# Expert weights stored by partition and column half, gathers that pass over empty places, and a landing allowance for the first expert

## The chip, the cores and the metric

One core of a Trainium2 chip runs the whole program in a single launch. The metric is the device time of that launch in microseconds, taken as the median of several executions; lower is better. One further execution was recorded by the hardware profiler, and the rows below come from that one. The engines are called as the profile calls them: PE (matrix), PEld (its weight load), DVE (vector), ACT (scalar), POOL (GpSimd) and SP (sync, which issues most DMAs).

## What is computed

A decoder layer over 2048 tokens of width 1024: an input projection, three parallel mixers (stick-breaking attention with 8 heads, a gated recurrence, a convolution module), an output projection, and then a mixture of experts. Only the last part matters here:

```python
logits_c = h @ w_coarse                      # 4 groups, take the best
logits_f = h @ w_fine                        # 8 experts a group, take the best two of the group
gate = softmax(top_val) * w_grp
# every token goes to 2 of 32 experts:
y[tok] += gate * ((silu(x[tok] @ w_gate[e]) * (x[tok] @ w_up[e])) @ w_down[e])
```

`w_gate` and `w_up` are 1024 x 512 for each expert, `w_down` is 512 x 1024, all float32: 2 MB each, 6 MB an expert, some 201 MB for 32 experts.

## The kernel before

**One plan for the whole program.** `Plan` collects every step as an `Op` with an engine, a cost, its reads and writes and a wished time, and then writes out a fixed order for every engine. `schedule` does it `ROUNDS` = 4 times: `forward` is a list scheduler that fills the engines by priority, `backward` runs the same from the end and gives every op a new priority (the latest end that it may have), so that the next `forward` follows other priorities everywhere; the best of the four orders is issued. On the chip each engine works through its own list in that order: an instruction whose input is late holds up whatever stands behind it on the same engine. A step that starts a DMA (`nb` bytes) is taken to land at `DMA0 + nb / DMAR + DMA1` after its issue, in ns; for one 512 KB piece of weights these constants come to 3.2 us.

**The order of the work.** The projection comes first, then attention. From attention's last steps on, the 16 token tiles of 128 tokens pass through `tok_tile` (norms, output projection L1286 to L1288, residual L1295, the second norm: square L1308 on ACT, root L1317 and L1319 on POOL, scaling L1335 on DVE, transposes L1354 on PE, router logits) and `route` (choice of experts, and a scatter of every token's place into the table `tab`, L1576). `provisional` looks at the counts after 12 of the 16 tiles and fixes one expert as the first (r = 0), so that its weights can be loaded, and its first 128 tokens worked on, while the last four tiles are still being routed. `order` ranks the others when routing is complete.

**An expert (`moe`).** Every expert has a fixed number of places (`ROOM`: from 256 down to 96, together 4864 places for 2048 x 2 = 4096 assignments); a place without a token has index 2048 or above and gate 0. For each expert, `reg` reads its number into an SP register, and twelve pieces of 512 KB are loaded: `gu` eight of gate and up, `dn` four of down. `piece` issues the DMA into one of the raw buffers (four, F5 to F8, for the first expert; eight later) on SP (L1743), lets ACT (`hi_act`, L388) or POOL (`hi_pool`, L391) round it to a high part and DVE (`lo`, L394) take the rest as a low part. `gather` loads the expert's slice of the table (L1796) and fetches the token rows, 4 KB each, by an indirect DMA from POOL (L1799); `split` transposes them on PE (L1818) and splits them. `down` ends in an indirect DMA that adds the rows to the output (L1964).

**Two ways through gate and up.** Where an expert has 129 to 192 places (`wide`, 15 experts, 120 pieces), `gate_up_wide` keeps the weights stationary, four K blocks by 256 columns a piece; there one DMA piece is, for each partition, four runs of 256 floats (1 KB). The other 17 experts (136 pieces, 20 tiles of at most 128 tokens) go through `gate_up`: the tokens are stationary and the weights move, two K blocks by all 512 columns a piece; there a piece is two runs of 2 KB for each partition, and the 256 rows of a piece lie in a row in HBM. A piece of down is one run of 4 KB.

`wts` and the rings tie experts to each other: a high or low buffer is written again when PE has done with the piece twelve places earlier, a raw buffer when DVE has.

Of the kernel before, what the change touches and what calls it, by code (L numbers as in the profile page):

```python
# [9 lines left out]
F32 = mybir.dt.float32  # L10
F32R = mybir.dt.float32r
BF16 = mybir.dt.bfloat16
I32 = mybir.dt.int32
# [6 lines left out]
P = 128  # L20
D = 1024
S = 2048
KD = D // P
NH = 8
HD = 64
NE = 32
# [53 lines left out]
TABLE = 1283  # L80
ROUNDS, LOOK = 4, 179.658
# [50 lines left out]
class Op:  # L132
    __slots__ = ("eng", "cost", "fn", "nb", "tab", "prio", "deps", "outs", "n", "ready", "end", "idx", "label", "start", "lk", "soft")


class Plan:
# [17 lines left out]
    def op(self, eng, cost, fn, r=(), w=(), nb=0, late=0, tab=None, lk=False, after=None):  # L154
        o = Op()
        o.eng, o.cost, o.fn, o.nb, o.tab, o.lk = eng, cost, fn, nb, tab, lk
# [97 lines left out]
    def forward(self, look):  # L254
# [3 lines left out]
        for o, push in self.pick([o for o in self.ops if not o.n], look):  # L258
# [4 lines left out]
            for p in o.outs:  # L263
                p.ready = max(p.ready, o.end if p.soft == o.idx else dma + DMA1 if o.nb else o.end + LAT[o.eng][p.eng])
                p.n -= 1
                if not p.n:
                    push(p.ready, p)
# [4 lines left out]
    def backward(self):  # L272
        for o in self.ops:
            o.n, o.ready, o.prio = len(o.outs), 0, -o.end
        for o, push in self.pick([o for o in self.ops if not o.n], 0):
            for i in o.deps:
                p = self.ops[i]
                p.ready = max(p.ready, o.end + (0 if o.soft == i else DMA0 + p.nb / DMAR + DMA1 if p.nb
# [32 lines left out]
class Kern:  # L311
# [1380 lines left out]
    def moe(self, TE, TX, TW, T5):  # L1692
# [43 lines left out]
        def piece(r, src, view):  # L1736
# [7 lines left out]
                         nb=1 << 19)  # L1744
# [15 lines left out]
        N2 = lambda ap: ap.rearrange("p (k f) -> p k f", k=2)  # L1760

        def gu(r, i0, i1):
            w = wts.setdefault(r, ([], [], []))
            for q in range(i0, i1):
                if not wide(r):
# [3 lines left out]
                        bass.ds(regs[r], 1), k * 256:(k + 1) * 256, :].rearrange("o (k p) f -> p (o k) f", p=P), N2))  # L1769
# [4 lines left out]
                    bass.ds(regs[r], 1), kh * 512:(kh + 1) * 512, fp * 256:(fp + 1) * 256].rearrange(  # L1774
                        "o (k p) f -> p (o k) f", p=P), K4))
# [6 lines left out]
        def gather(g):  # L1782

            r = g["r"]
# [3 lines left out]
            for off, n, at0 in ((g["off"], g["na"], (0,)), (g["off"] + P, g["nb"], (0, HD))):  # L1788
# [6 lines left out]
                for p0 in at0:  # L1795
# [5 lines left out]
                    in_offset=bass.IndirectOffsetOnAxis(ap=sl[:n, 0:1].bitcast(I32), axis=0)), sk[:1] + hs, (x,),  # L1801
# [25 lines left out]
        def gate_up(g):  # L1827
# [6 lines left out]
            for k in range(KD):  # L1834
                ps = [w[m][k // 2] for m in range(2)]

                def f(k=k, ps=ps):
                    for ac, (hi, lo) in zip(acc, ps):
                        wh, wl = (N2(v())[:, k % 2] for v in (hi, lo))
                        xh, xl = xv(k)[:, k % 4, 0], xv(k)[:, k % 4, 1]  # L1840
                        nc.tensor.matmul(ac()[:n], xh, wh, start=(k == 0), stop=False)  # L1841
                        nc.tensor.matmul(ac()[:n], xh, wl, start=False, stop=False)  # L1842
                        nc.tensor.matmul(ac()[:n], xl, wh, start=False, stop=(k == KD - 1))  # L1843
# [192 lines left out]
    def overflow(self):  # L2036
        nc, tc, a, scr = self.nc, self.tc, self.a, self.scr
        with ExitStack() as ctx:
# [3 lines left out]
            with tc.For_i(0, n, 1) as i:  # L2042
# [17 lines left out]
                for nm in ("wg", "wu"):  # L2060
                    w = sb.tile([P, KD, 512], F32, name=nm)
                    nc.sync.dma_start(w, a[nm][bass.ds(e, 1)].rearrange("o (k p) f -> p (o k) f", p=P))
# [130 lines left out]
```

## Time and profile before

| | us |
|---|---|
| median of 3 runs | 2123.84 |
| lowest, highest | 2121.97, 2129.23 |
| the profiled execution, its own time | 2134.14 |
| its span, first to last instruction | 2132.5 |

The page gives busy time by engine, a strip of the span in 40 slices, DMA queues, the chain that ended last and the costliest groups. Matmuls are pipelined, so a busy PE need not be PE at its peak; the granted clock says at which of two levels it ran (1.00 is 2.4 GHz, 0.50 is 1.2 GHz). The mean DMA share can pass 1, since packets in flight on one engine overlap.

### The profile page before, as it was taken

What the parts mean: (1) busy time and instruction counts of PE and PEld (TensorE: products, weight loads), DVE (VectorE), ACT (ScalarE), POOL (GpSimd) and SP (SyncE); (2) the same over time, 40 slices, a digit from 0 to 9 for tenths busy, and PEclk for the clock granted to TensorE, in tenths of its full rate; (3) what the DMA queues carried; (4) which work ended last, traced back from release to release, by engine and by line L of the source; (5) the groups of instructions that cost most, each with busy time, mean ns of one, the idle gap of its engine ahead of it and who ended that gap; (6) DMA issues with size and microseconds to landing.
All of it is one profiled execution on the core that took longest, in us unless ns stands there. A gap on an engine that the chain in (4) does not pass through costs nothing. (4 is left out here: it accounts for less than half of the span.)

```text
span 2132.5 us, 34284 instructions
## 1 busy us (share of the span) xinstructions
PE 1978.0 (93%) x10871; PEld 1644.3 (77%) x10871; DVE 1729.3 (81%) x2450; ACT 1270.4 (60%) x2332; POOL 1333.6 (63%) x1299
## 2 busy tenths in 40 slices
PE   6799998999889999999999977999999999999997
PEld 4678886888667887788888756778898887988776
DVE  7985579956799999898898757668898977888785
ACT  5434554456688988688787533446555555655554
POOL 6654777558876676766676533336676765757664
PEclk9899999999999999999999988999999999999999
DMA  5431361324875554578676556898999999999995
GB/s 185 155 111 55 114 183 60 134 84 134 238 225 158 170 162 142 115 202 231 187 212 192 147 130 195 288 280 262 300 305 313 302 311 283 323 288 283 295 310 136
DMA packets 316326, 437.21 MB, mean 205 GB/s; under 512 B 29424, under 2 KB 200816, under 8 KB 316144
## 3 DMA queue, kind: packets, MB, share of 16 engines
q1 hardware_dynamic: 303792, 395.12, 59.8%
q0 software_dynamic: 12352, 39.89, 8.1%
q8 instruction: 87, 1.43, 0.3%
q14 instruction: 95, 0.78, 0.1%
HBM read 360.95 MB, written 73.96 MB: 204 GB/s over the span
## 5 line engine op out<-in xcount | busy, mean ns | idle before, releaser
L394 DVE TENSOR_TENSOR R<-F,R 128x1024 fp32r<-128x1024 f32 (+1 forms) x390 | 493.0, 1285 | 111.9 <-ACT R L388 56.5
L874 PE MATMUL B<-R,R 128*128 128x512 f32 x1920 | 471.3, 402 | 33.4 <-DVE R L498 16.6
L874 PEld LDWEIGHTS B<-R,R 128*128 128x128 f32 x1920 | 363.6, 192 | 119.0 <-DVE R L498 18.3
L1050 POOL TENSOR_TENSOR F<-F,O 128x512 f32<-128x512 f32 (+2 forms) x320 | 314.0, 991 | 155.0 <-DVE O L1042 142.2
L391 POOL TENSOR_SCALAR R<-F 128x1024 fp32r<-128x1024 f32 (+2 forms) x181 | 200.5, 1116 | 157.7 <-DMA F<-in_wu 26.3
L1888 PE MATMUL B<-R,R 128*128 128x288 f32 (+3 forms) x960 | 269.1, 355 | 7.2 <-DVE O L1906 7.2
L388 ACT ACTIVATE R<-F 128x1024 fp32r<-128x1024 f32 (+1 forms) x209 | 210.0, 1022 | 75.9 <-DMA F<-in_wg 30.9
L1042 DVE TENSOR_TENSOR_SCAN O<-O,O,B 128x513 f32<-128x513 f32 x192 | 241.1, 1270 | 14.8 <-ACT O L1027 7.1
L1890 PE MATMUL B<-R,R 128*128 128x144 f32 (+3 forms) x960 | 217.9, 247 | 0.0
L1025 ACT ACTIVATE F<-B 128x512 f32<-128x512 f32 (+2 forms) x320 | 176.4, 555 | 56.2 <-PE B L1015 30.4
L1086 DVE TENSOR_TENSOR R<-B,R 128x512 fp32r<-128x512 f32 (+1 forms) x336 | 185.8, 572 | 20.8 <-ACT R L1078 19.6
L1078 ACT ACTIVATE R<-B 128x512 fp32r<-128x512 f32 (+1 forms) x336 | 172.9, 533 | 49.4 <-PE B L1070 40.8
L1888 PEld LDWEIGHTS B<-R,R 128*128 128x128 f32 x960 | 179.7, 194 | 10.6 <-issue 8.1
L1890 PEld LDWEIGHTS B<-R,R 128*128 128x128 f32 x960 | 183.5, 196 | 0.9
L1027 ACT ACTIVATE O<-B 128x512 f32<-128x512 f32 (+2 forms) x320 | 177.8, 559 | 0.2 <-PE B L1015 0.2
L1070 PE MATMUL B<-ident,F 128*128 128x128 f32 x1088 | 171.5, 276 | 2.7 <-DVE R L1086 2.4
L1964 POOL DMA_INDIRECT out<-F,sl x50 | 98.5, 1969 | 91.4 <-DVE F L1961 32.8
L1014 PE MATMUL B<-R,R 128*128 128x512 f32 (+2 forms) x320 | 131.5, 411 | 22.5 <-DMA R<-k 7.6
L1070 PEld LDWEIGHTS B<-ident,F 128*128 128x128 f32 x1088 | 129.2, 142 | 24.3 <-DVE R L1086 7.3
L394 DVE TENSOR_TENSOR R<-O,R 128x1024 fp32r<-128x1024 f32 x94 | 123.3, 1321 | 16.5 <-POOL R L391 12.3
L1104 PE MATMUL B<-R,R 128*128 128x256 f32 (+3 forms) x388 | 130.5, 348 | 5.1 <-DVE O L1116 4.2
L1105 PE MATMUL B<-R,R 128*128 128x256 f32 (+3 forms) x424 | 130.4, 320 | 0.7 <-DVE R L1086 0.6
(355 smaller groups left out, 4778.2 us busy)
## 6 DMA issues: line engine op xcount, KB each, us to landing
F<-in_wg SPq DMA_DIRECT2D x112, 512.0 KB
F<-in_wd SPq DMA_DIRECT2D x96, 512.0 KB
R<-k SPq DMA_DIRECT2D x336, 128.0 KB
F<-in_wu SPq DMA_DIRECT2D x82, 512.0 KB
R<-v SPq DMA_DIRECT2D x112, 256.0 KB
O<-in_wu SPq DMA_DIRECT2D x46, 512.0 KB
F<-in_w_in SPq DMA_DIRECT2D x80, 256.0 KB
O<-in_wd SPq DMA_DIRECT2D x32, 512.0 KB
```

The source lines that it names most:

```text
L388: self.nc.scalar.activation(out, in_, AF.Identity if not isinstance(scale, float) else AF.Copy, scale=scale)
L391: self.nc.gpsimd.tensor_scalar(out, in_, 1.0, 1.0, op0=ALU.mult, op1=ALU.mult)
L394: self.nc.vector.tensor_tensor(out, in_, f32(hi), op=ALU.subtract)
L874: nc.tensor.matmul(acc(), l_, r_, start=(k == 0 and j == 0), stop=(k == KD - 1 and j == 2))
L1025: op("ACT", c_act(wd), lambda: nc.scalar.activation(w()[:, :wd], z()[:, :wd], AF.Sigmoid, scale=0.125), (z,), (w,), tab="sig")
L1027: op("ACT", c_act(wd), lambda: nc.scalar.activation(kp()[:, o:QT], z()[:, :wd], AF.Sigmoid, scale=-0.125), (z,), (kp,), tab="sig")
L1042: nc.vector.tensor_tensor_scan(qb()[:, o:][:, ::-1], k, z()[:, 0:1].to_broadcast([P, wd + 1]), init, op0=ALU.mult, op1=ALU.bypass)
L1050: op("POOL", 1.77 * wd + 130, lambda: nc.gpsimd.tensor_tensor(w()[:, :wd], w()[:, :wd], qb()[:, o + 1:], op=ALU.mult), (qb,), (w,), lk=True)
L1070: nc.tensor.transpose(tp()[:, col:col + P], w()[:, c * P:(c + 1) * P], self.ident)
L1086: op("DVE", c_dve(a1 - a0), lambda: nc.vector.tensor_tensor(wl()[:, a0:a1], tp()[:, a0:a1], f32(wh()[:, a0:a1]), op=ALU.subtract), (tp, wh ...
L1888: big = lambda **st: nc.tensor.matmul(o()[:, :2 * n], K4(hi())[:, k, js], x.rearrange("p a t -> p (a t)"), **st)
L1890: sml = lambda **st: nc.tensor.matmul(o()[:, :n], K4(lo())[:, k, js], x[:, 0], **st)
```

## The change

Three edits. First, the host stores gate and up weights as `(expert, partition, column half, K block, 256)`; the pieces, the moving operand of `gate_up` and its output view follow, and so does the overflow path. A wide piece is then one run of 4 KB for each partition, and a narrow one still two runs of 2 KB; the partitions of one expert lie 16 KB from each other. Second, the gather of token rows is given a bound of `S - 1` and told that an index above it is no error: such rows aren't fetched, and the buffer keeps what it held. The scatter at the end still covers all places. Third, the plan takes the first expert's weights to land `LAG` = 8000 ns later than its constants say, in `forward` and in `backward`; nothing on the chip waits for that, only the order written out can differ.

```diff
+LAG = 8000
...
-                p.ready = max(p.ready, o.end if p.soft == o.idx else dma + DMA1 if o.nb else o.end + LAT[o.eng][p.eng])
+                p.ready = max(p.ready, o.end if p.soft == o.idx else dma + DMA1 + o.lag if o.nb else o.end + LAT[o.eng][p.eng])
...
-                p.ready = max(p.ready, o.end + (0 if o.soft == i else DMA0 + p.nb / DMAR + DMA1 if p.nb
+                p.ready = max(p.ready, o.end + (0 if o.soft == i else DMA0 + p.nb / DMAR + DMA1 + p.lag if p.nb
...
             last[0] = op("SP", 580, lambda: nc.sync.dma_start(view(raw()), src()), (("reg", r),) + hold, (raw,),
-                         nb=1 << 19)
+                         nb=1 << 19, lag=0 if r else LAG)
...
-        N2 = lambda ap: ap.rearrange("p (k f) -> p k f", k=2)
+        N2 = lambda ap: ap.rearrange("p (g k f) -> p g k f", g=2, k=2)
...
-                        bass.ds(regs[r], 1), k * 256:(k + 1) * 256, :].rearrange("o (k p) f -> p (o k) f", p=P), N2))
+                        bass.ds(regs[r], 1), :, :, 2 * k:2 * k + 2].rearrange("o p g k f -> p (o g) k f"), N2))
...
-                    bass.ds(regs[r], 1), kh * 512:(kh + 1) * 512, fp * 256:(fp + 1) * 256].rearrange(
-                        "o (k p) f -> p (o k) f", p=P), K4))
+                    bass.ds(regs[r], 1), :, fp, 4 * kh:4 * kh + 4].rearrange("o p k f -> p (o k) f"), K4))
...
-                    in_offset=bass.IndirectOffsetOnAxis(ap=sl[:n, 0:1].bitcast(I32), axis=0)), sk[:1] + hs, (x,),
+                    in_offset=bass.IndirectOffsetOnAxis(ap=sl[:n, 0:1].bitcast(I32), axis=0),
+                    bounds_check=S - 1, oob_is_err=False), sk[:1] + hs, (x,),
...
-                        wh, wl = (N2(v())[:, k % 2] for v in (hi, lo))
+                        wh, wl = (N2(v())[:, :, k % 2] for v in (hi, lo))
...
-                        nc.tensor.matmul(ac()[:n], xh, wh, start=(k == 0), stop=False)
+                        o = ac()[:n].rearrange("p (g f) -> p g f", g=2)
+                        nc.tensor.matmul(o, xh, wh, start=(k == 0), stop=False)
...
+    halves = lambda w: np.ascontiguousarray(w.reshape(NE, KD, P, 2, 256).transpose(0, 2, 3, 1, 4))
...
-        "wg": g["exp_w_gate"][0], "wu": g["exp_w_up"][0], "wd": g["exp_w_down"][0],
+        "wg": halves(g["exp_w_gate"][0]), "wu": halves(g["exp_w_up"][0]), "wd": g["exp_w_down"][0],
```

## Rows read from the trace of the kernel before

**Rows 1.** The page: its first line, and busy time, share of the span and number of instructions of each engine (one line of five).

```profile
span 2132.5 us, 34284 instructions
...
PE 1978.0 (93%) x10871; PEld 1644.3 (77%) x10871; DVE 1729.3 (81%) x2450; ACT 1270.4 (60%) x2332; POOL 1333.6 (63%) x1299
```

**Rows 2.** Busy time of the engines in stretches: the stretch and its length, busy us (and instructions) of PE, PEld, DVE, ACT, POOL, then the granted clock, the DMA share and GB/s. 0 to 650 is the projection and early attention, 650 to 1100 attention with token tiles, 1200 to 1300 the last four token tiles, 1300 to 2133 the experts, 1400 to 2100 the experts without start and end.

```profile
0.00:650.00 650.00, 583.98 (x2708) 467.27 (x2708) 498.46 (x711) 346.83 (x574) 436.92 (x463) 0.97 0.47 141
650.00:1100.00 450.00, 433.20 (x2710) 363.32 (x2709) 410.21 (x606) 369.94 (x787) 309.69 (x323) 0.99 0.62 171
...
1200.00:1300.00 100.00, 77.09 (x417) 62.47 (x415) 64.17 (x188) 32.34 (x60) 37.56 (x52) 0.88 0.53 138
1300.00:2133.00 833.00, 787.08 (x4390) 668.05 (x4390) 667.14 (x808) 442.01 (x745) 490.28 (x406) 0.98 0.90 283
1400.00:2100.00 700.00, 674.45 (x3857) 577.99 (x3858) 587.93 (x679) 393.53 (x669) 439.78 (x364) 0.98 0.95 297
```

**Rows 3.** The chain that ended last, in order of time, cut to 1195 to 1320: start, length, what.

```profile
1222.85 17.55 DMA F<-in_wu
1240.48 1.05 POOL R L391
1241.60 1.28 POOL r L1317
1242.95 0.59 POOL r L1319
1243.57 1.29 DVE F L1335
1244.91 1.12 PE B L1354 x4
```

**Rows 4.** Timeline of SP: start, length and line of three issues of the first expert's weights (the last line is three issues in one).

```profile
1218.54 0.41 SPq L1743 DMA_DIRECT2D F<-in_wg  x1
...
1221.06 1.09 SPq L1743 DMA_DIRECT2D F<-in_wg  x1
...
1287.58 3.64 SPq L1743 DMA_DIRECT2D F<-in_wd  x3
```

**Rows 5.** Timelines of DVE, ACT, POOL and PE in 1205 to 1325: start, length, line, operation; in brackets the idle time of that engine just before, and what ended it.

```profile
1230.26 0.69 DVE L1295 TENSOR_TENSOR F<-B,F 128x512 f32<-128x512 f32 x1 [1.86 <-PE B L1288]
1238.46 1.23 DVE L394 TENSOR_TENSOR R<-F,R 128x1024 fp32r<-128x1024 f32 x1 [7.51 <-ACT R L388]
...
1237.37 1.06 ACT L388 ACTIVATE R<-F 128x1024 fp32r<-128x1024 f32 x1 [8.34 <-DMA F<-in_wg]
1238.34 1.04 ACT L1308 ACTIVATE F<-F 128x1024 f32<-128x1024 f32 x1
...
1240.98 1.06 ACT L1268 ACTIVATE R<-F 128x1024 fp32r<-128x1024 f32 x1 [1.51 <-DVE F L1262]
...
1295.60 1.06 ACT L388 ACTIVATE R<-F 128x1024 fp32r<-128x1024 f32 x1 [3.35 <-DMA F<-in_wd]
...
1240.48 1.05 POOL L391 TENSOR_SCALAR R<-F 128x1024 fp32r<-128x1024 f32 x1 [10.29 <-DMA F<-in_wu]
...
1244.91 1.12 PE L1354 MATMUL B<-ident,F 128*128 128x128 f32 x4 [13.02 <-DVE F L1335]
...
1312.94 1.97 PE L1818 MATMUL B<-ident,F 128*128 128x128 f32 x8 [0.70 <-DMA F<-h,sl]
```

**Rows 6.** Stretches of 10 us in the same place, columns as in rows 2.

```profile
1230.00:1240.00 10.00, 1.87 (x7) 1.35 (x6) 2.23 (x3) 2.10 (x3) 0.19 (x1) 0.50 0.91 122
1240.00:1250.00 10.00, 5.09 (x20) 4.29 (x21) 5.76 (x7) 2.25 (x3) 4.01 (x4) 0.60 0.90 304
```

**Rows 7.** Waits in 1400 to 2100: who waited for whom, us in total, times, longest. The two largest of PE, and the largest of DVE.

```profile
PE B L1818 <- DMA F<-h,sl: 10.0, 6, 3.3
PE B L1888 <- DVE O L1906: 7.2, 6, 2.7
...
DVE R L394 <- POOL R L391: 41.5, 29, 5.4
```

**Rows 8.** DMA queues in 1400 to 2100: queue and kind, packets, MB, share of 16 engines' time in that stretch. q1 holds the DMAs that SP issues, q0 the indirect ones of POOL.

```profile
q1 hardware_dynamic: 112079, 174.67, 74.1%
q0 software_dynamic: 9280, 32.51, 20.1%
```

**Rows 9.** The same for the queue of SP in five short stretches that hold almost one size of run: 1806 to 1812 (1 KB, wide gate and up), 1632 to 1638 (2 KB, narrow gate and up), 1417 to 1420 and 1917 to 1923 (4 KB, down), 2 to 12 (2 KB, input and projection weights, whose rows lie 8 and 10 KB apart).

```profile
q1 hardware_dynamic: 1750, 1.74, 89.4%
...
q1 hardware_dynamic: 941, 1.79, 85.0%
...
q1 hardware_dynamic: 347, 1.26, 102.6%
...
q1 hardware_dynamic: 338, 1.19, 63.0%
...
q1 hardware_dynamic: 1101, 1.87, 57.3%
```

**Rows 10.** Groups of instructions by line and shape: busy us in all, mean ns of one, idle time before them. The narrow gate and up matmul (the first of its three lines), a matmul of the down product with the same shape, and the gathers.

```profile
L1841 PE MATMUL B<-R,R 128*128 128x512 f32 x160 | 64.6, 404 | 0.0
...
L1947 PE MATMUL B<-R,R 128*128 128x512 f32 x200 | 78.7, 394 | 0.0
...
L1799 POOL DMA_INDIRECT F<-h,sl x50 | 76.5, 1530 | 59.1 <-DMA sl<-tab 29.2 <-PE B L1948 12.0 <-issue 7.0
```

More of the change, by code (lines that the diff above doesn't have):

```diff
@@ L132 @@
 class Op:
-    __slots__ = ("eng", "cost", "fn", "nb", "tab", "prio", "deps", "outs", "n", "ready", "end", "idx", "label", "start", "lk", "soft")
+    __slots__ = ("eng", "cost", "fn", "nb", "tab", "prio", "deps", "outs", "n", "ready", "end", "idx", "label", "start", "lk", "soft", "lag")
 class Plan:
@@ L152, in at, with op @@
         self.n += 1
-    def op(self, eng, cost, fn, r=(), w=(), nb=0, late=0, tab=None, lk=False, after=None):
+    def op(self, eng, cost, fn, r=(), w=(), nb=0, late=0, tab=None, lk=False, after=None, lag=0):
         o = Op()
+        o.lag = lag
         o.eng, o.cost, o.fn, o.nb, o.tab, o.lk = eng, cost, fn, nb, tab, lk
@@ L1838, in f @@
                     for ac, (hi, lo) in zip(acc, ps):
-                        wh, wl = (N2(v())[:, k % 2] for v in (hi, lo))
+                        wh, wl = (N2(v())[:, :, k % 2] for v in (hi, lo))
                         xh, xl = xv(k)[:, k % 4, 0], xv(k)[:, k % 4, 1]
-                        nc.tensor.matmul(ac()[:n], xh, wh, start=(k == 0), stop=False)
-                        nc.tensor.matmul(ac()[:n], xh, wl, start=False, stop=False)
-                        nc.tensor.matmul(ac()[:n], xl, wh, start=False, stop=(k == KD - 1))
+                        o = ac()[:n].rearrange("p (g f) -> p g f", g=2)
+                        nc.tensor.matmul(o, xh, wh, start=(k == 0), stop=False)
+                        nc.tensor.matmul(o, xh, wl, start=False, stop=False)
+                        nc.tensor.matmul(o, xl, wh, start=False, stop=(k == KD - 1))
                 pe(6 * c_mm(512) + 30, f, [(g["xt"][k // 4], a_, 0) for a_ in range(2)] + list(ps[0] + ps[1]), acc,
@@ L2060, in overflow @@
                 for nm in ("wg", "wu"):
-                    w = sb.tile([P, KD, 512], F32, name=nm)
-                    nc.sync.dma_start(w, a[nm][bass.ds(e, 1)].rearrange("o (k p) f -> p (o k) f", p=P))
+                    w = sb.tile([P, 2, KD, 256], F32, name=nm)
+                    nc.sync.dma_start(w, a[nm][bass.ds(e, 1)].rearrange("o p g k f -> p (o g) k f"))
                     pg = ps.tile([P, 512], F32, name="p" + nm)
                     for k in range(KD):
-                        nc.tensor.matmul(pg, xt[:, k], w[:, k], start=(k == 0), stop=(k == KD - 1))
+                        nc.tensor.matmul(pg.rearrange("p (g f) -> p g f", g=2), xt[:, k], w[:, :, k], start=(k == 0),
+                                         stop=(k == KD - 1))
                     acc.append(pg)
```

## The prediction

> **What bounds the kernel now.** First the page's head: PE is busy 1978.0 of 2132.5 us [rows 1], and no other engine passes 81%. An average over stages says little, so next the stretches [rows 2]. In the experts without start and end (1400 to 2100) PE is busy 674.45 of 700 us, DVE 588, and the DMA share is 0.95: PE sets the pace, with DMA close behind. PE stands idle there for 25.5 us, and the granted clock is 0.98; if all of the missing 2% is time at 1.2 GHz, that costs another 0.02 x 700 = 14 us. These 39 us are all that faster transfers can give back in that stage. From 1200 to 1300, the last token tiles, PE is idle for 22.9 us in only 100, and the clock is 0.88.
>
> Most of the latter is one hole. The chain [rows 3] shows a DMA of the first expert's up weights landing 17.55 us after its issue, then POOL's rounding of it, and only then the root of token tile 13's second norm (L1317, L1319), its scaling (L1335) and the transposes (L1354). The timelines [rows 5] show that the token work had been ready: its residual ended at 1230.26 + 0.69 = 1230.95. Its square (L1308) stood behind an L388 that waited 8.34 us for gate weights, its root behind an L391 that waited 10.29 us, and DVE was in an L394 that had waited 7.51 us. PE was idle for 13.02 us, and then started at 1.2 GHz: the granted clock was 0.50 from 1230 to 1240 and 0.60 in the next 10 us [rows 6].
>
> **The change part by part.** *The allowance.* The plan took a piece to land 3.2 us after its issue; the two late ones were issued at 1221.06 [rows 4] and 1222.85 [rows 3] and were used at 1237.37 and 1240.48 [rows 5], after 16.3 and 17.6 us. With 8 us more the plan expects 11.2 us, that is 1232 to 1234, so it puts the rounding behind token work that it expects before that. Without the three weight steps in front, the hole would close like this: residual done 1230.95, square 1.04 and 0.2 for its sum to 1232.2, root 1.28 + 0.59 and a hand-over to 1234.2, scaling 1.29 to 1235.6, PE at about 1235.8 instead of 1244.91: 9.1 us less. The other bound is nothing: the allowance is still 5 to 6 us short of the landing, and one weight step left in front of tile 14's rounding (L1268, ready at about 1233.5 then) would hold the next matmuls to about 1240 and leave 4 to 5 us. I take 6 us, between the two and nearer to the full row. The displaced steps (two L388, L391, three L394, about 1.1 us each) move into a stretch in which ACT is busy 32% and POOL 38% [rows 2]: they cost nothing there; were that cover gone, some 3 us on DVE. Everything up to the loads of the second expert hangs on the last tiles' routing, so the gain should be kept.
>
> The same allowance makes the plan wrong for later pieces: of the three issued from 1287.58 on [rows 4] the last was being rounded at 1295.60 after a wait [rows 5], 4 to 8 us after issue. That is the rival below.
>
> The plan is also made anew as a whole, since `backward` hands out other priorities from that point back to the start. What it does in the projection and attention can't be read from this trace: PE is idle there for 66 us of 650 and 16.8 of 450 [rows 2], and an equally good order may win or lose some of it. I take 0, with 10 us either way in the range.
>
> *One run of 4 KB instead of four of 1 KB.* 120 pieces of 0.524 MB are 62.9 MB. The price is the share times the stretch over the MB [rows 9]: 1 KB runs cost 0.894 x 6 / 1.74 = 3.08 us of all 16 engines a MB, 2 KB runs 0.850 x 6 / 1.79 = 2.85, 4 KB runs 1.026 x 3 / 1.26 = 2.44 in an undisturbed stretch and 0.630 x 6 / 1.19 = 3.18 in a disturbed one. So the edit is worth between 62.9 x 0.64 = 40 us of DMA time and a loss of 6. I take the middle of the 4 KB rows, 2.8: 18 us. The Trainium skill (DMA: Bandwidth & Descriptors, Why small descriptors are slow) states a fixed overhead of about 3 cycles a packet, beside 32 cycles for 1 KB; by it 140 cycles become 131 and the estimate would be 6.4% of 62.9 x 3.08 = 194 us, 12 us; the rows differ by more in both directions.
>
> *Gathers.* At least 4864 - 4096 = 768 rows of 4 KB, 3.1 MB, aren't fetched. POOL's queue costs 0.201 x 700 / 32.51 = 4.3 us a MB [rows 8], in which the adding scatters are included; with the 4 KB price of 2.8 as the other bound that is 9 to 13 us. I take 9. Whether the bound makes the instruction itself dearer, the trace can't show: the 50 gathers take 1.53 us each [rows 10]; I take 0, up to 0.3 us each, 15 us of POOL, which is busy 63% of the stage, or as much less for fewer rows.
>
> *Narrow pieces and their matmuls.* The run stays 2 KB, but the partitions lie 16 KB apart instead of next to each other. The nearest rows with spaced partitions, at the start of the program, cost 0.573 x 10 / 1.87 = 3.06 us a MB against 2.85 [rows 9]: 136 pieces, 71.3 MB, up to 15 us of DMA time lost. A gain has no row; I take 0, as that stretch also holds the start-up. The moving operand now has two runs of 256 columns: 960 matmuls (20 tiles x 48); two lines of one shape differ by 404 - 394 = 10 ns [rows 10], so up to 10 us lost; I take 0, since 256 columns are read without a break.
>
> *What the DMA time is worth.* 18 + 9 = 27 us of about 665 (0.95 x 700). PE's own waits decide what passes through: 10.0 of 25.5 us name the gathers, 7.2 us name DVE's adds (L1906) [rows 7], which queue behind L394 on DVE, which waited 41.5 us for POOL's rounding. Only waits that name a DMA shrink for certain; the gathers' 10.0 is some 0.4 of PE's idle time, and they won't vanish at a share of 0.91. I pass 0.3 of it on: 8 us, of a ceiling of 39.
>
> **Sum.** The profiled execution took 2134.14 us (span 2132.5): 2134 - 6 - 8 = 2120. It lies 10.3 us above the median of the runs; 2123.84 - 14 gives **2110**.
>
> **The rivals.** *Only the hole closes* (0.20): PE is the bound among the experts and the DMA time is hidden anyway. For it: PE waits for hardly any weights by name. Against: the gathers do end PE waits. 2118. *The transfers were the bound* (0.08): all 27 us pass, and the hole gives 9: 2088. For it the DMA share of 0.95; against it the ceiling of 39, which would have to go almost whole. *The allowance delays the first expert* (0.13, slower): its twelve pieces go through four raw buffers, so the plan adds 8 us in each of up to three rounds, although the late rounds land in 4 to 8 us; rounding is put behind routing, and PE, in order, waits for weights that lie in SBUF. Slack before it decides: PE went into the second half of the first expert with an idle time of 0.70 us, ended by the gather [rows 5]; if the first half ends later than that gather lands, everything behind slips. One round too many costs 8 + 6 us against the forecast: 2124; two 2132. I take 2132. *Spaced partitions are slower* (0.07): the 16 KB step makes the narrow pieces as dear as at the start of the program (15 us lost), the wide ones gain nothing; 9 - 15 = -6 us of DMA time costs 2 us and the hole gives 6: 2120. The Trainium skill (DMA: Bandwidth & Descriptors, Latency and other measured facts) has a rule that speaks against this layout: row pitches at large powers of two lose rate, 207 GB/s at 512 KiB and 103 at 4 MiB; no run here shows a pitch of that size, and 16 KB lies far below its table. *The new order decides* (0.10): the gains are there, but 10 us are won or lost before 1200: 2100 or 2122.
>
> **How the numbers follow.** The forecast has 0.42, its own range being 2099 to 2119 (the hole 0 to 9, the experts 4 to 17, with a few us of order). Within 0.3% of 2123.84, about what a measurement of this kernel can tell from no change, is 2117.5 to 2130.2. Faster: most of the forecast (0.37), half of "only the hole" (0.09), the transfers (0.08), half of the new order (0.05), a little of the spaced partitions (0.01): 0.60. Slower: the larger part of the delay (0.10) and what a bad order adds to other cases (0.04): 0.14. The rest, 0.26, is no difference. For 8 in 10 the range runs from 2092 to 2131.
>
> **What would show it.** Right: the chain no longer has the 17.55 us DMA with L391 behind it; L1308 and L1317 of tile 13 run before the first expert's L388 and L391; PE's idle time from 1200 to 1300 falls from 22.9 to about 15; the packets of SP's queue fall by some 46,000; the DMA share from 1400 to 2100 falls to about 0.91, and PE's waits for gathers with it. Wrong: the hole stays with another weight step in front; PE waits for L394 between the last tile and the second expert; 4 KB packets cost over 3 us a MB; or the strip before 1200 has moved by more than the sum.

## The result, and the profile after

The changed kernel takes 2139.21 us (median of 4 runs, 2137.79 to 2140.96). The kernel before, run again beside it, has 2122.9 (median of 4). The ratio is 1.0070, 95% interval 1.0045 to 1.0095: **slower by 0.7%, some 15 us**, where 2110 was forecast, with 2092 to 2131 as the range. The profiled execution is one of those runs, 2137.79 us.

The page after, its first line and the line of busy times, beside [rows 1]:

```profile
span 2136.1 us, 34329 instructions
PE 1989.2 (93%) x10871; PEld 1650.3 (77%) x10871; DVE 1723.5 (81%) x2450; ACT 1267.9 (59%) x2332; POOL 1339.0 (63%) x1299
```

Line numbers after, and in e1_lag, are two to four higher than before, since lines were added above: ACT's rounding is L391 instead of L388, POOL's L394 instead of L391, DVE's low part L397 instead of L394, and SP's issue of weights L1746 instead of L1743. Three stretches after, columns as in [rows 2]:

```profile
1200.00:1300.00 100.00, 82.60 (x390) 65.24 (x389) 62.02 (x197) 28.96 (x54) 36.01 (x51) 0.85 0.48 132
1300.00:2133.00 833.00, 787.30 (x4368) 666.09 (x4366) 656.03 (x782) 440.89 (x743) 494.83 (x402) 0.97 0.88 279
1400.00:2100.00 700.00, 673.17 (x3830) 573.73 (x3829) 577.12 (x674) 388.62 (x662) 444.84 (x362) 0.99 0.91 291
```

The DMA queues after, 1400 to 2100, beside [rows 8]:

```profile
q1 hardware_dynamic: 65486, 173.06, 71.7%
q0 software_dynamic: 9275, 29.88, 19.1%
```

Most of the signs that the prediction named for itself are there. PE's idle time from 1200 to 1300 fell from 22.9 to 17.4 us, where about 15 was named; the DMA share among the experts fell from 0.95 to 0.91; in the whole program the packets of SP's queue fell from 303,792 to 257,712. One is missing: PE's waits for gathers from 1400 to 2100 did not fall with the share. They were 10.0 us [rows 7] and are now

```profile
PE B L1821 <- DMA F<-h,sl: 11.8, 5, 3.2
```

And the time went up. So the signs that came true were not the ones that decide.

Where it went is read from SP's issues of weights, since they mark the same places in both kernels. SP's timeline before, the first issue of the second expert and the last of the last (the very first one, 1218.54, is in [rows 4]):

```profile
1311.03 0.38 SPq L1743 DMA_DIRECT2D F<-in_wg  x1
...
2096.61 0.35 SPq L1743 DMA_DIRECT2D O<-in_wd  x1
```

The same three places after:

```profile
1210.94 0.68 SPq L1746 DMA_DIRECT2D F<-in_wg  x1
...
1303.33 0.56 SPq L1746 DMA_DIRECT2D F<-in_wg  x1
...
2100.61 0.33 SPq L1746 DMA_DIRECT2D O<-in_wd  x1
```

From the first expert's first issue to the second's: 92.5 us before, 92.4 after. In these two profiles the closed hole gave nothing in sum. From there to the last issue, which I call **the expert stretch**: 785.6 before, 797.3 after, 11.7 us more. That is where the loss sits. The start of the stretch before differs too (1218.54 and 1210.94), but that is scatter: the fifteen profiles below that follow the very order of the kernel before begin between 1205.0 and 1215.8. The 10 us by which the profiled execution of before lay above its median are at least in part of this kind.

### The profile page after: what moved, and what is told of

Read it like the earlier page. It is cut to its first block, busy times and chain, and to the rows that moved or that the text cites. A ratio compares the mean times of both kernels' runs of the same rounds, so it can differ in the third digit from the quotient of the medians.

```text
span 2136.1 us, 34329 instructions
## 1 busy us (share of the span) xinstructions
PE 1989.2 (93%) x10871; PEld 1650.3 (77%) x10871; DVE 1723.5 (81%) x2450; ACT 1267.9 (59%) x2332; POOL 1339.0 (63%) x1299
## 3 DMA queue, kind: packets, MB, share of 16 engines
q0 software_dynamic: 12352, 36.74, 7.7%
## 4 chain that ended last, share of the span: by engine, by line
PE 51%; DVE 14%; DMA 14%; issue 8%; POOL 6%; ACT 6%; SPq 1%; DVEq 0%; POOLq 0%; ACTq 0%
PE B L877 11%; DVE R L397 5%; PE B L1073 4%; PE B L1892 4%; DMA F<-in_wu 2%; PE B L1017 2%; PE B L1107 2%; PE B L1108 2%; PE B L1845 2%; PE B L1846 2%; PE B L1847 2%; PE B L1018 2%; PE B L1950 2%; PE B L1289 2%; PE B L1952 2%
## 5 line engine op out<-in xcount | busy, mean ns | idle before, releaser
L397 DVE TENSOR_TENSOR R<-F,R 128x1024 fp32r<-128x1024 f32 (+1 forms) x390 | 492.1, 1282 | 114.5 <-POOL R L394 59.4
L394 POOL TENSOR_SCALAR R<-F 128x1024 fp32r<-128x1024 f32 (+2 forms) x181 | 204.0, 1132 | 146.3 <-PE B L877 26.1
L391 ACT ACTIVATE R<-F 128x1024 fp32r<-128x1024 f32 (+1 forms) x209 | 209.9, 1022 | 83.3 <-DMA F<-in_wg 36.3
L1968 POOL DMA_INDIRECT out<-F,sl x50 | 97.3, 1947 | 101.1 <-DVE F L1965 35.1
L397 DVE TENSOR_TENSOR R<-O,R 128x1024 fp32r<-128x1024 f32 x94 | 121.0, 1295 | 25.6 <-POOL R L394 15.7
```

Source lines behind the costliest of these rows:

```text
L391: self.nc.scalar.activation(out, in_, AF.Identity if not isinstance(scale, float) else AF.Copy, scale=scale)
L394: self.nc.gpsimd.tensor_scalar(out, in_, 1.0, 1.0, op0=ALU.mult, op1=ALU.mult)
L397: self.nc.vector.tensor_tensor(out, in_, f32(hi), op=ALU.subtract)
```

## The experiments

Neither the storage nor the bound changes a cost in the plan, so every engine's order follows from the allowance alone. Theory A: that order is what costs. Rivals: B, the storage; C, the bound. Each ratio below is to the kernel before, run on the same chip in turn with it.

**Allowance alone (e1_lag).**

```diff
-                         nb=1 << 19)
+                         nb=1 << 19, lag=0 if r else LAG)
```

> The kernel before with the allowance of 8000 ns alone; the order of every engine is then that of the changed kernel, while the weights and the gathers stay as they were. Theory A (the new order is what costs): the changed kernel is 16 us slower although it moves 3.1 MB less in gathers and 62.9 MB in cheaper packets, so this one has the loss without those gains: 2139 to 2150 us. Theory B (the layout is what costs: its issues take 0.54 us instead of 0.37 on SP, its partitions lie 16 KB apart): the order closes the hole and the layout is not there, so 2110 to 2118. Theory C (the bound makes the gathers dearer): 2110 to 2118 as well.

Measured 2131.38 against 2131.05: 1.0006 (0.9982 to 1.0030).

**Storage alone (e2_layout).** The diff of the change without `LAG` and without the bound.

> The kernel before with the new storage of gate and up alone, in the order of before, with unbounded gathers. Theory A: the packets are cheaper and nothing else differs, so 2105 to 2123 us. Theory B: 2130 to 2145, with the rounding waiting longer for in_wg and in_wu than before. Theory C: 2105 to 2123.

Measured 1.0086 (1.0054 to 1.0119), some 18 us.

**Bound alone (e3_bound).**

```diff
+                    bounds_check=S - 1, oob_is_err=False), sk[:1] + hs, (x,),
```

> The kernel before with the bound on the gathers alone. Theory A and B: 3.1 MB less in POOL's queue, worth at most the 9 to 13 us of DMA time, of which some 0.3 pass: 2117 to 2123 us. Theory C: each of the 50 gathers takes longer on POOL or lands later than its 1.53 us and the waits of 12 us, and the time is 2130 or above.

Measured 0.9994 (0.9973 to 1.0014).

**Storage and bound, no allowance (e4_nolag).**

```diff
-LAG = 8000
+LAG = 0
```

> The changed kernel with the allowance set to 0: storage and bound together, in the order of before. Theory A: both gains and not the loss, 2095 to 2120 us, and below the kernel before by more than 0.3%. Theory B or C: 2130 to 2140, close to the changed kernel, and then the order is not the cause.

Measured 1.0068 (1.0040 to 1.0096). Theory A, with which I began, fell: allowance and bound are each worth nothing that can be told, and the storage carries the whole loss. The next question is which part of it. For these runs the host holds a second copy of gate and up, so that wide and narrow experts can be loaded from different storages; the control for that copy is further down.

**Wide pieces alone from the new storage (e5_wide).**

```diff
-                w[m].append(piece(r, lambda nm=("wg", "wu")[m], fp=fp, kh=kh: a[nm][
-                    bass.ds(regs[r], 1), kh * 512:(kh + 1) * 512, fp * 256:(fp + 1) * 256].rearrange(
-                        "o (k p) f -> p (o k) f", p=P), K4))
+                w[m].append(piece(r, lambda nm=("wg", "wu")[m], fp=fp, kh=kh: a[nm + "h"][
+                    bass.ds(regs[r], 1), :, fp, 4 * kh:4 * kh + 4].rearrange("o p k f -> p (o k) f"), K4))
```

> The kernel before, with a second copy of gate and up in the new storage from which the 15 wide experts alone are loaded (one run of 4 KB for each partition, 16 KB apart); the narrow ones keep the old storage. Theory P (the 16 KB step from partition to partition is what delays the landing): part of the loss, 5 to 15 us above the kernel before. Theory R (the long runs themselves delay what is queued behind them): the whole loss, 14 to 22 us above. Theory I (the narrow pieces are what costs, by issues of 0.54 us on SP instead of 0.37 and a moving operand in two parts): no loss, 0 to 5 us below the kernel before.

Measured 1.0024 (1.0006 to 1.0043), 5 us: the low end of theory P. R expected far more, and I no loss.

**Narrow pieces alone from the new storage (e6_narrow).** The same, the other way round: gate and up as `halves`, the wide pieces from a copy in the old storage.

> The reverse: narrow experts from the new storage with the two-part operand, wide ones from a second copy in the old storage (four runs of 1 KB). Theory P: part of the loss, 5 to 15 us above the kernel before. Theory R: no loss, within 4 us of it. Theory I: the whole loss, 14 to 22 us above.

Measured 1.0069 (1.0046 to 1.0092), 14.7 us: the upper end of theory P and the lower end of I. R, with no loss here, is refuted.

**Wide pieces as blocks of 512 KB (e7_wide4k).**

```diff
+                w[m].append(piece(r, lambda nm=("wg", "wu")[m], fp=fp, kh=kh: a[nm + "h"][
+                    bass.ds(regs[r], 1), fp, kh].rearrange("o p f -> p (o f)"), lambda ap: ap))
```

> The kernel before with a second copy of gate and up in which each wide piece is one block of 512 KB: again one run of 4 KB for each partition, but the partitions lie 4 KB apart, as in a piece of down. Narrow pieces as before. Theory P: no loss and perhaps the gain that the prediction hoped for, 0 to 10 us below the kernel before. Theory R: 14 to 22 us above, as with the 16 KB step. Theory I: 0 to 5 us below.

Measured 1.0018 (0.9998 to 1.0038), 4 us above, which none of the three expected. The long runs give no gain, with 4 KB from partition to partition as little as with 16.

**Storage alone, padded to 17 KB (e8_pad).**

```diff
+    halves = lambda w: np.concatenate([w.reshape(NE, KD, P, 2, 256).transpose(0, 2, 3, 1, 4).reshape(NE, P, -1),
+                                       np.zeros((NE, P, 256), np.float32)], axis=2)
```

> The new storage alone, as in the run with storage alone (18.6 us above the kernel before), but with 1 KB of padding behind each partition, so that the partitions lie 17 KB apart instead of 16; runs, packets, issues and matmuls stay the same. Theory P, if the power of two is what hurts: 0 to 6 us above the kernel before, or below it. Theories R and I, and P if distance alone hurts: unchanged, 14 to 22 us above.

Measured 1.0051 (1.0033 to 1.0069), 11 us, between the expectations. By e5_wide and e6_narrow most of the loss belongs to the narrow pieces. Padding seems to take a part of it away, but this interval still overlaps that of e2_layout; e11_npad and e18_afterpad below have to show it. Three things differ in a narrow piece: the distance of the partitions, the operand in two parts, the longer issue. Four runs for these:

**Same DMA, operand in one part (e9_plain).**

```diff
+    spaced = lambda w: np.ascontiguousarray(w.reshape(NE, 4, 2, P, 512).transpose(0, 3, 2, 1, 4))
...
+                        bass.ds(regs[r], 1), :, :, k].rearrange("o p j f -> p (o j) f"), N2))
```

> The kernel before, with the narrow experts loaded from a second copy in which a piece is again two runs of 2 KB, 8 KB from each other, with the partitions 16 KB apart, as in the changed kernel; but K blocks instead of column halves are what lies apart, so that the moving operand stays in one part, and the source is written in three dimensions instead of four. Narrow pieces alone from the new storage cost 14.7 us. Theory P (the 16 KB step): again 10 to 19 us above the kernel before. Theory O (the moving operand in two parts): no loss, within 4 us. Theory I (0.54 us of SP for an issue): no loss if the issue takes 0.37 us here, 10 to 19 us if it takes 0.54.

Measured 1.0049 (1.0025 to 1.0072), 10 us, with an issue of 0.54 us. Theory O expected no loss; P is left, and so is I.

**Pieces in blocks, operand in two parts (e10_twopart).**

```diff
+    blocks = lambda w: np.ascontiguousarray(w.reshape(NE, 4, 2, P, 2, 256).transpose(0, 1, 3, 4, 2, 5)).reshape(NE, 4, P, 1024)
```

> The reverse: narrow pieces from a second copy in which each is one block of 512 KB (one run of 4 KB for each partition, 4 KB apart), in the order column half, K block, column, so that the moving operand lies in two parts. Theory P: no loss, within 4 us of the kernel before. Theory O: 10 to 19 us above. Theory I: no loss, as an issue of one run takes 0.33 us.

Measured 1.0024 (0.9999 to 1.0048), 5 us. The operand isn't it: the loss stays without the two parts, and is small with them.

**Narrow pieces, padded to 17 KB (e11_npad).** The run of narrow pieces alone, with the padding of e8_pad.

> Narrow experts from the new storage as in the run of narrow pieces alone (14.7 us above the kernel before, 2 KB packets at 101.8 ns), with 1 KB of padding behind each partition: 17 KB instead of 16; wide ones from the old storage. Theory P: the packets come back to some 98 ns and the loss to 0 to 7 us. Theories O and I: unchanged, 10 to 19 us above.

Measured 1.0022 (1.0000 to 1.0045), 5 us, the 2 KB packets at 97.0 ns, the issue at 0.37 us, as theory P expected.

**Source in fewer dimensions (e12_merged).**

```diff
+                        bass.ds(regs[r], 1), :, :, k].rearrange("o p g f -> p (o g) f"), G2))
```

> Narrow experts from the new storage, wide ones from the old, as in the run of narrow pieces alone, byte for byte, but the two adjacent dimensions of the source (K block, column) are written as one. If that brings the issue on SP from 0.54 back to 0.37 us: theory I has no loss, within 4 us of the kernel before, and theories P and O have 10 to 19 us as before. If the issue stays at 0.54, all three expect 10 to 19 us, and the issue stays undecided by this run.

Measured 1.0078 (1.0052 to 1.0104), issue still 0.54 us: the way in which the source is written doesn't matter.

Padding had healed issue and packets together. Either 16 KB is the trouble, or that it is exactly twice the 8 KB between a piece's two runs, so that its 256 runs are evenly spaced.

**16 KB, not evenly spaced (e13_step4).**

```diff
+    spaced = lambda w: np.ascontiguousarray(w.reshape(NE, 2, 2, 2, P, 512).transpose(0, 4, 1, 3, 2, 5))
...
+                        bass.ds(regs[r], 1), :, k // 2, :, k % 2].rearrange("o p j f -> p (o j) f"), N2))
```

> Narrow experts from a second copy with partitions 16 KB apart and two runs of 2 KB a piece, as in the plain-operand run (8 us above the kernel before, issue 0.54 us, 2 KB packets at 103.5 ns), but the two runs lie 4 KB from each other instead of 8, so that the step from partition to partition is no longer twice the step inside one. Theory B (the distance of 16 KB itself slows the reads): packets over 101 ns and 6 to 14 us above the kernel before. Theory C (16 KB is exactly twice 8 KB, so the 256 runs of a piece become one evenly spaced list, which is issued in 0.54 us and handed out to the DMA engines in another way): issue at 0.37 us, packets at 97 to 98 ns, and within 4 us of the kernel before.

Measured 1.0026 (1.0007 to 1.0045), 5.5 us, with packets at 97.2 ns and an issue of 0.37 us. Packets and issue are as theory C expected; the time lies between the two.

**Evenly spaced, 17 KB (e14_uniform17).**

```diff
+    spaced = lambda w: np.concatenate([w.reshape(NE, 4, 2, P, 512).transpose(0, 3, 2, 1, 4).reshape(NE, P, 2, 2048),
+                                       np.zeros((NE, P, 2, 128), np.float32)], axis=3)
```

> The reverse: partitions 17 KB apart, the two runs of a piece 8.5 KB from each other, so that the step is again exactly twice as large, and no power of two. Theory B: issue at 0.37 us, packets at 97 to 98 ns, within 5 us of the kernel before, as with padding behind the partition (2.2 of 1000 above it). Theory C: issue at 0.54 us, packets over 101 ns, 6 to 14 us above.

Measured 1.0029 (1.0008 to 1.0049), 6 us. Issues of SP from 1380 to 1740 in three runs; after the count: shortest, median, longest in ns, first and last start in us. `in_wgh` and `in_wuh` are the second copy, for the narrow pieces. First e9_plain:

```profile
L1743 SPq DMA_DIRECT2D F<-in_wuh x21: 542/543/577, 1382.2 to 1738.5; - x21
```

e13_step4:

```profile
L1743 SPq DMA_DIRECT2D F<-in_wuh x21: 372/373/1057, 1384.4 to 1731.7; - x21
```

e14_uniform17:

```profile
L1743 SPq DMA_DIRECT2D F<-in_wuh x22: 542/543/1073, 1380.0 to 1735.5; - x22
```

Even spacing makes the issue long at either distance. The packets don't follow it: 103.5, 97.2 and 98.4 ns. Theory B is refuted by the packets of e13_step4 and theory C by those of e14_uniform17, since each expected over 101 ns there; the time of e14_uniform17 lies at the edge of both ranges and decides nothing. Each theory is half right. The issue depends on even spacing. Of the steps tried, the packets are slow at the even step of 8 KB alone, and narrow pieces cost 0.49 to 0.78% with it (e6, e9, e12) and 0.22 to 0.29% without it (e10, e11, e13, e14). Some of these intervals overlap one by one; it is the three against the four that tells them apart.

**Allowance and bound, old storage (e15_lagbound).**

> The kernel before with allowance and bound, and the old storage. If the parts add up, 0.06% and -0.06% give no difference: 2124 us within 0.3%, and 15 us below the changed kernel. If the bound needs the new order (or the order the shorter gathers) to pay, 2 to 10 us below the kernel before.

Measured 0.9992 (0.9971 to 1.0013): the parts add up to nothing.

**Half of the wide loads (e16_half).**

```diff
-                    bass.ds(regs[r], 1), kh * 512:(kh + 1) * 512, fp * 256:(fp + 1) * 256].rearrange(
-                        "o (k p) f -> p (o k) f", p=P), K4))
+                    bass.ds(regs[r], 1), kh * 512:kh * 512 + 256, fp * 256:(fp + 1) * 256].rearrange(
+                        "o (k p) f -> p (o k) f", p=P), lambda ap: K4(ap)[:, :2]))
```

> What DMA time is worth here. The kernel before, with each of the 120 wide pieces loading only its first two K blocks, 256 KB in place of 512; the other half of the buffer keeps what it held, so the wide experts compute with stale weights; all other work is the same. 31.5 MB less, some 97 us of the 16 engines by the price of the 1 KB runs (3.08 us a MB). If DMA time passes at 0.3, as predicted for the experts, 25 to 30 us below the kernel before. If the transfers are hidden and only the landing of single pieces counts, 0 to 10 us below.

Measured 0.9987 (0.9966 to 1.0009). 1400 to 2100 of that run, columns as in [rows 2], and the wait of PE for gathers, to be held against [rows 7]:

```profile
1400.00:2100.00 700.00, 677.54 (x3911) 578.88 (x3910) 596.10 (x689) 394.20 (x680) 450.19 (x372) 0.99 0.82 250
```

```profile
PE B L1818 <- DMA F<-h,sl: 3.0, 3, 1.5
```

The DMA share falls by 0.13, PE's waits for gathers by 7 us, PE's idle time from 25.5 to 22.5 us, and the time doesn't change by more than can be told. In the packets the saving is 94 us: from 1300 to 2100 the 1 KB packets take 98 us of all 16 engines instead of 192. The 97 us of the expectation were worth 2.8 us at best guess, 0.03 and not 0.3; the interval allows 7 us, 0.07.

**Control: a second copy stored as the first (e17_copy).**

> A control for the runs with a second copy of gate and up: the kernel before, in which the narrow experts are loaded from a second copy that is stored exactly as the first. Seven kernels with a second copy came out 0.18% to 0.29% above the kernel before where neither issue nor packets were slow. If the copy itself costs that: 0.2% above the kernel before, some 2129 us, and then wide pieces in long runs and narrow ones off the even 8 KB step cost nothing of their own. If the copy is free: within 0.1% of the kernel before, and each change of the storage costs some 5 us.

Measured 0.9997 (0.9977 to 1.0017). At best guess the copy is free, and the interval leaves it 0.17% at most. (The expectation counts seven kernels; those above are five, e5, e7, e10, e11 and e13, and e14 with its slow issue as a sixth.)

**The changed kernel, padded (e18_afterpad).** The padding of e8_pad in the whole change.

> The whole changed kernel, with 1 KB of padding behind each partition of gate and up. If the parts add up, it keeps the 0.51% that the padded storage alone cost, less 0.08% for allowance and bound: 0.3% to 0.6% above the kernel before, 2130 to 2136 us, and some 0.3% below the changed kernel. If the even 8 KB step is all that the storage costs in the new order: within 0.2% of the kernel before.

Measured 1.0024 (1.0004 to 1.0043): of the changed kernel's 0.70% a third is left, between the two expectations. It is not faster than the kernel before, and no version that I tried is by more than can be told.

All runs together. The expert stretch is read from SP's timeline as above; the 2 KB packets are the mean of all of SP's from 1300 to 2100 in the trace (none in e10_twopart); the issue is the median of a narrow piece.

| run | ratio | expert stretch, us | 2 KB packet, ns | issue, us |
|---|---|---|---|---|
| before | 1 | 785.6 | 96.1 | 0.37 |
| e3 bound; e1 allowance; e15 both | 0.9994; 1.0006; 0.9992 | 784.2; 785.5; 786.7 | 97.6; 97.8; 96.3 | 0.37 |
| e17 control; e16 half loads | 0.9997; 0.9987 | 788.6; 781.8 | 97.1; 96.9 | 0.37 |
| e5 wide 4 KB at 16 KB; e7 at 4 KB | 1.0024; 1.0018 | 796.0; 790.6 | 97.3; 96.8 | 0.37 |
| e10 narrow blocks | 1.0024 | 790.1 | - | 0.33 |
| e11 narrow at 17 KB; e13 uneven at 16 KB | 1.0022; 1.0026 | 784.1; 785.8 | 97.0; 97.2 | 0.37 |
| e14 narrow even at 17 KB | 1.0029 | 793.3 | 98.4 | 0.54 |
| e8 storage at 17 KB; e18 with all | 1.0051; 1.0024 | 789.6; 791.5 | 98.1; 97.0 | 0.37 |
| e9, e6, e12 narrow, even 8 KB step | 1.0049; 1.0069; 1.0078 | 797.3; 800.3; 791.6 | 103.5; 101.8; 101.4 | 0.54 |
| e2 storage; e4 with bound | 1.0086; 1.0068 | 803.9; 803.6 | 101.4; 101.4 | 0.54 |
| changed kernel | 1.0070 | 797.3 | 100.2 | 0.54 |

The ratios are of many executions, the stretches of one each, and the two do not always go together: e12_merged has a ratio of 1.0078 with 791.6 us, e5_wide one of 1.0024 with 796.0. Where they differ, the ratio counts.

## Why the prediction was wrong, point by point

**The allowance: mechanism right, "the gain should be kept" wrong.** Square and root of tile 13 do run before the rounding now, and PE's hole is 2.89 us in place of 13.02 [rows 5]. ACT, POOL and PE after:

```profile
1220.99 1.06 ACT L1311 ACTIVATE F<-F 128x1024 f32<-128x1024 f32 x1 [1.36 <-DVE F L1298]
...
1222.23 0.22 POOL L1320 TENSOR_SCALAR r<-s 128x1 f32<-128x1 f32 x1 [1.63 <-ACT F L1311]
...
1224.48 1.11 PE L1357 MATMUL B<-ident,F 128*128 128x128 f32 x4 [2.89 <-DVE F L1338]
...
1228.93 1.06 ACT L391 ACTIVATE R<-F 128x1024 fp32r<-128x1024 f32 x1 [2.71 <-DMA F<-in_wg]
```

What is late next is seen best in e1_lag, where only the order differs. POOL, DVE and PE there:

```profile
1237.81 1.12 POOL L1802 DMA_INDIRECT F<-h,sl  x1 [13.64 <-DMA sl<-tab]
1238.97 1.08 POOL L394 TENSOR_SCALAR R<-F 128x1024 fp32r<-128x1024 f32 x1
```

```profile
1240.09 1.23 DVE L397 TENSOR_TENSOR R<-F,R 128x1024 fp32r<-128x1024 f32 x1 [8.13 <-POOL R L394]
...
1245.91 0.22 DVE L1518 TENSOR_TENSOR OH<-E 128x64 bf16<-128x64 f32 x1
```

```profile
1246.19 0.21 PE L1549 MATMUL B<-OH,tri 128*128 128x32 bf16 x2 [5.44 <-DVE OH L1518]
1249.62 1.44 PE L1245 MATMUL B<-o,F 128*128 128x1 f32 x6 [1.34 <-DVE d L1531]
```

The displaced rounding on POOL now stands behind the first gather, which waits 13.64 us for its slice of the table; DVE's low part waits 8.13 us for that rounding, the routing of tile 13 stands behind it, and PE waits for the routing's one-hot matrix. The changed kernel has the same wait, 12.11 us. Its chain shows what the slice was late for, the scatter of places into the table, which landed 13.58 us after its start:

```profile
1218.63 13.58 DMA tab<-ent,dst
1232.23 2.16 DMA sl<-tab
```

One late DMA was exchanged for another on the same in-order engines. The step that failed is "they cost nothing there": it rested on busy shares of 32 and 38% of a stretch, and not on what stands in the queue in front. The rival "the allowance delays the first expert" comes near, but it had rounding behind routing, where the trace has routing behind rounding, and its price was too high. From the first issue to the second expert's the pairs that differ in the allowance alone take 92.5 us without and 92.3 with it (before, e1_lag), 93.6 and 89.7 (e3_bound, e15_lagbound), 95.4 and 92.4 (e4_nolag, changed kernel). Up to 4 us may be gained there, of the 6 that I took, but single profiles without the allowance scatter from 91.2 to 96.8, and none of the three pairs has a ratio that shows a gain: 1 and 1.0006, 0.9994 and 0.9992, 1.0068 and 1.0070.

**The transfers: sized right, worth next to nothing.** 4 KB packets take 45.8 ns a KB in place of 50.2 for 1 KB, 9% of the 192 us that the latter took from 1300 to 2100, or 17 us of DMA time, against the 18 taken; the gathers fetch 3.15 MB less (39.89 to 36.74 in the whole program), and the 3.1 were right. What failed is the factor: "I pass 0.3 of it on". e16_half measured it at 0.03, 0.07 at most. I had read the factor from PE's waits for gathers, and there they fell from 10.0 to 3.0 us without as much as that in the time. A share of 0.95 looked like a bound next to PE's; it was a full queue whose late pieces cost little. They did come late: from 1400 to 2100 the rounding on ACT and POOL waited 66.6 us for weights before and 35.6 in e16_half, and the time did not follow. Of the ceiling of 39 us, faster packets of the wide pieces had at most 7 within reach. The rival "the transfers were the bound" goes with this. "Only the hole closes" was right in that the DMA time is hidden, and wrong about the hole. Fewer bytes in the narrow pieces were not tried; longer runs in them (e10_twopart) gained nothing.

**Narrow pieces: "I take 0" is the step that put the sign wrong.** They cost 0.69%, 14.7 us. The bound that I gave, up to 15 us of DMA time lost, held: 208.6 us of 16 engines for the 2 KB packets in e6_narrow against 198.6 in e11_npad, 10 us. But I priced it as I priced the gains, at 0.3, and the rival of spaced partitions came to 2 us where the chip shows 15. It had the right place, the spacing of the narrow pieces, though not the step that matters, and a chance of 0.07. Mean DMA time is the wrong measure in both directions: taking 97 us of it away gave 3, adding 10 in this way took 15. How the loss comes about shows where it is largest, from the second expert's first issue to that of the 17th expert: the same work, 389.3 us before and 402.9 after. The two stretches, columns as in [rows 2], before:

```profile
1311.00:1700.30 389.30, 375.91 (x2032) 319.96 (x2033) 314.21 (x365) 208.02 (x338) 218.21 (x174) 1.00 0.93 295
```

After:

```profile
1303.30:1706.20 402.90, 382.95 (x2020) 325.25 (x2021) 310.15 (x366) 206.16 (x336) 221.31 (x174) 0.97 0.89 281
```

Of the 13.6 us more, 6.6 are idle time of PE (13.4 to 20.0), and 7.0 are busy time: the same matmuls take longer, and the granted clock fell from 1.00 to 0.97, so that part of them ran at the lower of its two levels. The same stretch in the control has 390.3 us and a clock of 1.00. In the rest of the expert stretch the sides change (396.3 us at 0.97 before, 394.4 at 0.98 after), so one profile each isn't enough. Over the whole expert stretch it holds in all of them: PE is idle for 30.2 to 33.6 us and busy for 752.2 to 755.4 in the five profiles with the old storage (before, e1, e3, e15, e17), idle for 34.1 to 41.9 and busy for 757.5 to 763.2 in the six with the even 8 KB step (changed kernel, e2, e4, e6, e9, e12). The four with narrow pieces off that step (e10, e11, e13, e14) are nearer to the old storage, with 28.0 to 35.2 and 755.3 to 758.1. The waits of ACT's rounding for gate weights in these stretches, before:

```profile
ACT R L388 <- DMA F<-in_wg: 11.2, 7, 5.2
...
ACT R L388 <- DMA O<-in_wg: 6.3, 3, 3.4
```

After:

```profile
ACT R L391 <- DMA F<-in_wg: 20.9, 11, 7.6
...
ACT R L391 <- DMA O<-in_wg: 15.9, 4, 5.7
```

Over all weights ACT's and POOL's rounding waits 49.8 us before and 75.9 after. The other profiles of the two groups have 42 to 56 and 54 to 72 in this stretch, and from 1400 to 2100 they have 63 to 74 and 75 to 101, with 75 to 80 in e10, e11, e13 and e14. So pieces land after they are needed more often. That DVE's low part and PE stand still behind this rounding, and that the gaps cost clock as well, fits the lines but isn't shown: in e16_half half of these waits went away and gave next to nothing.

The landing itself can be read from the traces, which keep sixteen landing signals for a piece (here for pieces issued from 1300 to 2100 with at least fourteen of them on record). From the start of its issue to its last signal a narrow piece takes 7.6 to 7.9 us on average in the six kernels with the even 8 KB step, 6.6 to 7.0 in the old storage, 6.7 to 6.8 with 1 KB of padding, and 7.1 and 7.2 in e13_step4 and e14_uniform17. So it lands some 1 us later. Packets that are 5 ns dearer account for less than 0.1 us of it (an estimate: 256 packets on 16 engines, 16 x 5 ns). From the first signal to the last it is 2.4 to 2.7 us with the even step and 1.8 to 2.1 in the old storage, which would fit slow packets that crowd on some of the 16 engines; but e13_step4 has 2.4 as well without the loss. Why whole pieces come so much later stays open.

The rule of the Trainium skill that I weighed against the layout (DMA: Bandwidth & Descriptors, Latency and other measured facts: row pitches at large powers of two lose rate, and padding brings it back) points the right way at 16 KB, far below its table, which is of copies between HBM tensors: 1 KB of padding brought the packets from 101.8 to 97.0 ns. But a pitch of 16 KB alone didn't do it (97.2 ns in e13_step4); here it took an even step of 8 KB.

**Operand and bound: 0, and right but for a little in the bound.** The narrow matmul with all 128 rows takes, from 1300 on, 406, 402 and 401 ns on its three lines in e6_narrow, 399, 394 and 393 in e9_plain, 402, 396 and 394 in e10_twopart, which has the two parts too. The gathers take 1.53 to 1.60 us each in the five kernels with the bound and 1.48 to 1.57 in the others, 0.05 more on average: 3 us of POOL, and in e3_bound the time shows none of it.

**The plan made anew: 0, and right.** e1_lag puts its whole effect at 0.06%.

**What stays open.** The wide pieces in long runs, narrow blocks, and narrow pieces off the 8 KB step each cost about 0.2%, with intervals that end near 0, and the copy is hardly the reason: the control puts it at -0.03% (0.17% at most), and e18_afterpad, which has no copy, is left with 0.24% too. PE's named waits from 1400 to 2100 are 25 to 30 us in them, against 25 to 27 with the old storage (before, e1, e3, e15, e17) and 26 to 37 with the even 8 KB step, and no one wait stands out.

## What to carry to other kernels

A DMA share near 1 says that the queue is full, not that the end hangs on it: before paying for cheaper transfers, halve some loads and see whether the time moves. When a layout is chosen, look at the step between all runs of one DMA, not only at their length: an even step of 8 KB cost more here than runs four times as long could give, and 1 KB of padding took 40 to 70% of it back (e2 to e8, e6 to e11, the changed kernel to e18). And a step that is moved away from a late DMA has to be followed to the instruction that it now stands behind.

## What the runs showed that I had not expected

- An issue on SP takes 0.54 us and not 0.37 when the 256 runs of a piece are evenly spaced, taken partition by partition (8 or 8.5 KB), however the source is written. By itself it costs nothing that can be told: e14_uniform17 and e13_step4, timed together, have 1.0029 and 1.0026.
- 2 KB packets take 100 to 104 ns at an even step of 8 KB, and 96 to 99 ns in the old storage, at 8.5 KB, at 17 KB with 8 KB inside, and at 16 KB with 4 KB inside. Of even steps between narrow runs, only 8 and 8.5 KB were tried.
- Runs of 4 KB in place of 1 KB for a third of the weights lower the DMA time by 9% of their part and gain nothing.
- One and the same order reaches the first expert between 1205.0 and 1218.5 us from one profiled execution to the next, while the expert stretch of the old storage with full loads repeats within 784.2 to 788.6.
